# Raw weights in one tile with five places, and one split for the sums of two neighbouring quads

## The chip, the cores and the metric

The kernel runs on one core of a Trainium2 chip. The time is what the device takes for one execution, in microseconds (us). The engines work side by side, each through its own instructions in a fixed order, and wait for one another through semaphores: TensorE (PE) multiplies matrices, VectorE (DVE) and ScalarE (ACT) work element by element, GpSimd (POOL) and SyncE (SP) mostly issue DMA transfers here.

## The reference

One layer of a decoder trunk on 256 tokens of width 2048, in float32:

```
x = x + 0.5 * SwiGLU_1(RMSNorm(x))         # 2048 -> 5632 -> 2048
h = RMSNorm(x)
[attn q,k,v | m q,k,v,o,i,f] = h @ W_in    # one projection
y = concat(differential attention, mLSTM)
x = x + y @ W_out
x = x + 0.5 * SwiGLU_2(RMSNorm(x))
out = RMSNorm(x)
```

Nearly all of the work is products of activations (256 rows) with weights that are read once from memory.

## The kernel before

**Splits.** Float32 accuracy comes from two parts of each operand. A weight block `raw` is split by `split` (line 131): ACT casts it to a rounded upper half `hi` (line 132), and DVE subtracts that from the source to get the lower half `lo` (line 133). A product then takes three matmuls (`mms`, line 177): both halves of the activations with `hi` (lines 181 and 182), and the upper half of the activations with `lo` (line 184). The split weights go into pairs of tiles from the pool `wsp`, four deep.

**Seven products instead of eight.** `Paired` (line 422) multiplies the same activations with two weight arrays `wa` and `wb`. For the first `ns` pairs of contraction blocks it uses a scheme with sums in the manner of Winograd. Such a pair of blocks with its weights is called a quad here. `load` (line 440) brings three 128 x 512 pieces of a quad into a tile `raw` of the pool `wr`, which has five buffers: slot 0 from `wa`, slots 1 and 2 from `wb`. The fourth piece (`late`, line 506) comes later into another pool. The raw pieces are then added to each other in place, and between the additions the sums are split and multiplied, two quads at a time (`twos`, line 429; with an odd number the last quad is alone):

- `leading` (line 468): load; A1, the split of slot 0 as loaded; then DVE adds slots 0 and 2 to slot 1's piece (line 479, writing slots 0 and 1).
- `second_sum` (line 488): S1, the split of slot 0; then slot 2 is added to slot 0, by a DMA from POOL's queue (line 495) where `by_dma` is set and it is not the last of `twos`, by DVE otherwise (line 497).
- `sums` (line 521): S2, the split of slot 0; then POOL's queue adds `late` to slot 0 by DMA (line 533); `bare`, the split of `late`; S3, the split of slot 1.
- `second` (line 559): for each quad one split of slots 0 and 2 with a stride (line 562), the last use of the quad's buffer.

A1, S1, S2 and S3 go through `part` (line 462), which calls `split_two` (line 451): for two quads it makes two casts and two subtractions of 128 x 512, into the two halves of one pair of `wsp` tiles.

**The rest.** The contraction blocks beyond the quads are plain units: a 128 x 1024 piece from the pool `wrp` is split by one cast and one subtraction and used in twelve matmuls (`plain`, line 548). `Chain.run` (line 608) interleaves the `leading` of a Paired with the last plain units (`third`) of the one before.

**Order.** The instructions are traced under a planner that orders each engine's work by priority. Loads and splits stand 400 steps ahead of their place (`AHEAD`), so that they run ahead of the matmuls as far as buffers allow. A few copies out of the accumulators are put ahead of splits by counting splits (`ahead_of_splits`, `split_weights`, line 150). Loads of quads are issued from POOL's queue (from SP's in the first three chunks), those of plain units and of `late` from SP's.

Two more users of the pool `wr` exist, at the very start only: `tile_by_tile` (line 230) and the spare units of `load_unit` (line 212), together four buffers in the first gate product.

The Paired products in order, by number of quads: first feed-forward layer 3, 5, then two of 3, then 5, 5, two of 2, 5, 5, 5, two of 3, 5, 5, 5, two of 3; the mixing stage 2, 3, 5, 5, 5, 3 and the output projection 3, 3; second feed-forward layer 5, 5, 5, two of 3, 5, 5, two of 2, 5, 5, 5, two of 3, 5, 5, 5, two of 3.

Of the kernel before, what the change touches and what calls it, by code (L numbers as in the profile page):

```python
# [9 lines left out]
F32 = mybir.dt.float32  # L10
# [7 lines left out]
P = 128  # L18
# [6 lines left out]
CW = 512  # L25
# [7 lines left out]
UK = 2  # L33
# [10 lines left out]
AHEAD = 400  # L44
# [5 lines left out]
ON_POOL = 3  # L50
FIRST_SUMS = 3
FLUSH = 3

SEEDED = N11, N21 = "n11", "n21"

# [5 lines left out]
def tile_trunk_layer(ctx: ExitStack, tc: tile.TileContext, x, xt, par, bias_if, lamv, fnorm,  # L61
                     wg1, wu1, wd1, wqk0, wqk1, wqk2, win, wout, wg2, wu2, wd2, out):
    nc = tc.nc
# [1 line left out]
    big = ctx.enter_context(tc.tile_pool(name="big", bufs=1))  # L65
    slots = ctx.enter_context(tc.tile_pool(name="slots", bufs=22))
    work = ctx.enter_context(tc.tile_pool(name="work", bufs=8))
    wr = ctx.enter_context(tc.tile_pool(name="wr", bufs=5))
    wrp = ctx.enter_context(tc.tile_pool(name="wrp", bufs=5))
    wsp = ctx.enter_context(tc.tile_pool(name="wsp", bufs=4))  # L70
    small = ctx.enter_context(tc.tile_pool(name="small", bufs=2))
    ps_acc = ctx.enter_context(tc.tile_pool(name="ps_acc", bufs=4, space=PSUM))
    ps_tr = ctx.enter_context(tc.tile_pool(name="ps_tr", bufs=2, space=PSUM))

    wqk = [wqk0, wqk1, wqk2]
    uid = [0]

    def nm(s):
        uid[0] += 1
        return f"{s}_{uid[0]}"  # L80
# [47 lines left out]
        nc.vector.scalar_tensor_tensor(lo, src, prm[:, gcol:gcol + 1], hi.bitcast(F32),  # L128
                                       op0=ALU.mult, op1=ALU.subtract)

    def split(src, hi, lo):
        return (nc.scalar.copy(hi, src),  # L132
                nc.vector.tensor_tensor(out=lo, in0=src, in1=hi.bitcast(F32), op=ALU.subtract))  # L133


# [1 line left out]
    splits, queued = [], ([], [])  # L137

    def after(late, early):

        tc.add_manual_dep(late.ins, early.ins.name,
                          mybir.DependencyInfo(mybir.DependencyClass.NoSync, mybir.DependencyReason.DATA),
                          reason="order")
# [3 lines left out]

    ahead = ([], [])

    def split_weights(src, hi, lo):  # L150
        made = split(src, hi, lo)
        for late, q, past in zip(made, queued, ahead):
            while q and len(splits) >= q[0][0]:
                past.append(q.pop(0)[1])
            del past[:-3]
            for early in past:
                after(late, early)
        return made


    def pair_tiles(pool, tag, shape):
        return (pool.tile(shape, F32R, tag=tag + "h", name=nm(tag + "h")),
                pool.tile(shape, F32R, tag=tag + "l", name=nm(tag + "l")))
# [13 lines left out]
    def mms(jobs):  # L177


        for acc, lh, ll, rh, rl, first, last, on in jobs:  # L180
            nc.tensor.matmul(acc, lh, rh, start=first, stop=False, skip_group_check=on)  # L181
            nc.tensor.matmul(acc, ll, rh, start=False, stop=False, skip_group_check=on)  # L182
        for acc, lh, ll, rh, rl, first, last, on in jobs:
            newest[:] = [nc.tensor.matmul(acc, lh, rl, start=False, stop=last, skip_group_check=on)]  # L184
# [15 lines left out]
    def flush(n=None):  # L200

        now = pending[:n]
        del pending[:n]
        for f in now:
            f()

    def load_pair(dst, w, k, queue=nc.sync):
        queue.dma_start(dst, w[k // LK][:, k % LK:k % LK + 2, :])

    def load_unit(w, k, pieces=(UK,), spare=False):  # L210
        n = w.shape[3]
        if spare:
            raw = wr.tile([P, 3, n], F32, tag="raw", name=nm("raw"))[:, 0:UK, :]
        else:
            raw = wrp.tile([P, UK, n], F32, tag="rawp", name=nm("rawp"))
        with tc.high_priority(offset=AHEAD):
            o = k % LK
            for m in pieces:
                nc.sync.dma_start(raw[:, o - k % LK:o - k % LK + m, :], w[k // LK][:, o:o + m, :])
                o += m  # L220
        return raw
# [3 lines left out]
    def in_turn(load):  # L225
        for early in turns[-1:]:
            after(load, early)
        turns.append(load)

    def tile_by_tile(w, ahead):  # L230
        raw = wr.tile([P, 3, w.shape[3]], F32, tag="raw", name=nm("raw"))
        hi, lo = pair_tiles(wsp, "w", [P, UK, w.shape[3]])
        with tc.high_priority(offset=AHEAD):
            for t in range(UK):
                ahead(0, t)
                in_turn(nc.sync.dma_start(raw[:, t, :], w[0][:, t, :]))
                made = split_weights(raw[:, t, :], hi[:, t, :], lo[:, t, :])
        splits.append(made)
        ahead(1)
        return hi, lo  # L240

    def units(accs, xp, w, nk, last_units=1, ahead=None, w0=0, banks=None):
# [16 lines left out]
        for u in range(nu):  # L259
            if u == FLUSH:  # L260
                flush()
            if u == 0 and ahead is not None:
                rh, rl = tile_by_tile(w, ahead)
                for t in range(UK):
                    mms([(accs[hb], *halves(xp, t, hb), rh[:, t, :], rl[:, t, :], t == 0 and not (one and hb),
                          False, one) for hb in range(NT)])
                yield
                continue
            if ahead is not None and u % 2 == 0:
                ahead(u)  # L270
                ahead(u + 1)
            rh, rl = split_w(load_unit(w, w0 * LK + u * UK, (UK,), ahead is not None and u % 2 == 0), (UK,))
            if u < nu - last_units:
                products((0, 1), u, rh, rl)
            else:
                products((0,), u, rh, rl)
                tail.append((u, rh, rl))
            if u < nu - 1:
                yield
# [47 lines left out]
    A1, B1, A2, B2, S3, S1, S2, S4 = range(8)  # L327
# [7 lines left out]
    def sum_pair(xp, j, g, put_off=False):  # L335
        plain_pair(xp, j, "xs")
        split(g, *xp[j])
        (side.append if put_off else lambda f: f())(functools.partial(sums, g, xp, j))

    def sums(g, xp, j):  # L340
        s = wk("xsum").rearrange("p (a b) -> p a b", b=P)
        tt = nc.vector.tensor_tensor
        tt(out=s[:, 0:2, :], in0=g[:, 0:2, :], in1=g[:, 1:4:2, :], op=ALU.subtract)
        tt(out=s[:, 2, :], in0=s[:, 1, :], in1=g[:, 0, :], op=ALU.subtract)
        tt(out=s[:, 3, :], in0=g[:, 2, :], in1=s[:, 2, :], op=ALU.add)
        t = slots.tile([P, 2, 4, P], F32R, tag="s", name=nm("xs"))
        xp[j] += t[:, 0, :, :], t[:, 1, :, :]
        split(s, *xp[j][2:])
# [52 lines left out]
    class Early:  # L401


        def __init__(self, engine):
            self.engine = engine
# [16 lines left out]
    class Paired:  # L422

        def __init__(self, xp, wa, wb, nk, ns, w0=0, queue=nc.gpsimd, by_dma=True):

            self.queue, self.by_dma = queue, by_dma and ns > 3
            self.xp, self.wa, self.wb, self.k0 = xp, wa, wb, w0 * LK
            self.ns, self.rest = ns, range(2 * ns, nk, UK)
            self.twos = [range(j, min(j + 2, ns)) for j in range(0, ns, 2)]

            self.n = wa.shape[3]
            self.off = self.n - wb.shape[3]
            self.raws = []

        def job(self, acc, j, xi, w, wi, first, last, on=False):
            xh, xl = self.xp[j][2 * (xi // 4):][:2]
# [2 lines left out]

        def load(self, j):  # L440
            n, off = self.n, self.off
            raw = wr.tile([P, 3, n], F32, tag="raw", name=nm("raw"))
            self.raws.append(raw)
            k = self.k0 + 2 * j
            with tc.high_priority(offset=AHEAD):
                self.queue.dma_start(raw[:, 0, :], self.wa[k // LK][:, k % LK, :])
                load_pair(raw[:, 1:3, off:], self.wb, k, self.queue)
                if off:
                    nc.gpsimd.memset(raw[:, 1:3, 0:off], 0.0)

        def split_two(self, srcs):
# [7 lines left out]
                splits.append(made)  # L459
            return t  # L460

        def part(self, js, acc, xi, slot, first=False, last=False):

            t = self.split_two([self.raws[j][:, slot, :] for j in js])
            mms([self.job(acc, j, xi, t, i, first and j == 0, last and j == self.ns - 1, not first)
                 for i, j in enumerate(js)])

# [80 lines left out]
        def plain(self, w, k, accs, apart=False):  # L548

            rh, rl = split_w(load_unit(w, self.k0 + k), (UK,))  # L550

            def products(hbs):
                mms([(accs[hb], *halves(self.xp, k + t, hb), rh[:, t, :], rl[:, t, :],
                      False, k + t == self.rest[-1] + UK - 1, True) for hb in hbs for t in range(UK)])

            products((0,) if apart else (0, 1))
            return functools.partial(products, (1,))
# [481 lines left out]
    for hb in range(NT):  # L1039
        for h in range(NH):  # L1040
            i = hb * NH + h
# [226 lines left out]
```

## Time and profile before

| | |
|---|---|
| median of three runs | 1759.46 us (1758.83 to 1760.01) |
| profiled execution | 1759.56 us |
| its span, first to last instruction | 1757.8 us |
| mean granted TensorE clock | 0.999 |
| busy: PE, DVE, ACT, POOL | 1744.6, 1617.8, 1267.4, 429.3 us |
| instructions | 24486 |

Busy time is the time in which an engine has an instruction under way. A busy PE isn't PE at its peak, since matmuls are pipelined: a record is longer than the distance to the next one. Idle time of an engine that doesn't set the end costs nothing.

### The profile page before, as it was taken

To read this page: it belongs to the slowest core of one execution; us is meant where nothing else is said; L and a number is where in the kernel's file an instruction comes from. 1 tells how busy PE (TensorE), PEld (TensorE's weight loads), DVE (VectorE), ACT (ScalarE), POOL (GpSimd) and SP (SyncE) were. 2 spreads that over 40 slices of the span, in tenths; PEclk is the share of its full clock that TensorE was granted. 3 is DMA by queue.
4 is the path that set the end of the run, shared out by engine and by line. 5 is a ranking of instruction groups with operands and counts; after the bars stand their busy time and mean duration, and the time that the engine had idled before them with its cause. 6 is when DMAs were issued, how large, how long until landed. Compare 5 with 4: busy or idle time off the path is not lost.

```text
span 1757.8 us, 24486 instructions
## 1 busy us (share of the span) xinstructions
PE 1744.6 (99%) x7926; PEld 1437.7 (82%) x7926; DVE 1617.8 (92%) x2189; ACT 1267.4 (72%) x1949; POOL 429.3 (24%) x630
## 2 busy tenths in 40 slices
PE   9999999999999999999999999999999999999998
PEld 7788888888888888987888888888888878888886
DVE  7999999999999999898888999999999999999997
ACT  8666777777677768777687777776777677677765
POOL 0022332322233312012231101122332332233310
PEclk9999999999999999999999999999999999999999
DMA  9787998999799977577886667898998999799973
GB/s 365 251 254 209 259 261 265 253 292 265 218 262 258 263 252 204 185 230 221 236 238 192 209 210 211 260 265 233 258 260 268 241 268 276 232 246 256 283 254 115
DMA packets 155265, 429.72 MB, mean 244 GB/s; under 512 B 17632, under 2 KB 18944, under 8 KB 154880
## 3 DMA queue, kind: packets, MB, share of 16 engines
q0 software_dynamic: 76304, 196.66, 45.1%
q1 hardware_dynamic: 77680, 229.40, 38.0%
q10 hardware_dynamic: 1152, 2.09, 0.3%
q8 instruction: 62, 1.02, 0.2%
q14 instruction: 67, 0.55, 0.1%
HBM read 349.56 MB, written 2.10 MB: 200 GB/s over the span
## 4 chain that ended last, share of the span: by engine, by line
PE 93%; DMA 2%; DVE 2%; issue 1%; ACT 0%; POOL 0%; SPq 0%; POOLq 0%; DVEq 0%; ACTq 0%
PE acc L184 18%; PE acc L181 18%; PE acc L182 18%; PE accn L181 12%; PE accn L182 12%; PE accn L184 12%; DVE wl L133 1%; DMA raw<-in_wg_dram 1%; PE tr L373 1%; DMA raw<-in_wu_dram 1%; PE tr L314 0%; PE sc L1060 0%; DMA rawp<-in_wg_dram 0%; ACT wh L132 0%; PE num L1011 0%
## 5 line engine op out<-in xcount | busy, mean ns | idle before, releaser
L132 ACT CAST wh<-raw 128x512 fp32r<-128x512 f32 (+2 forms) x885 | 601.5, 708 | 214.5 <-PE acc L182 66.3
L133 DVE TENSOR_TENSOR wl<-raw,wh 128x512 fp32r<-128x512 f32 (+2 forms) x885 | 676.1, 793 | 58.4 <-ACT wh L132 54.5
L132 ACT CAST wh<-rawp 128x1024 fp32r<-128x1024 f32 (+3 forms) x308 | 318.2, 1035 | 109.5 <-PE acc L182 55.1
L133 DVE TENSOR_TENSOR wl<-rawp,wh 128x1024 fp32r<-128x1024 f32 (+3 forms) x308 | 367.1, 1197 | 32.0 <-ACT wh L132 29.8
L181 PE MATMUL acc<-wh,xs 128*128 128x512 f32 (+2 forms) x956 | 369.5, 387 | 0.0
L182 PE MATMUL acc<-wh,xs 128*128 128x512 f32 (+2 forms) x956 | 368.9, 386 | 0.0
L184 PE MATMUL acc<-wl,xs 128*128 128x512 f32 (+2 forms) x956 | 317.6, 387 | 0.8 <-DVE wl L133 0.7
L533 POOL DMA_DIRECT2D raw<-late x176 | 152.6, 1053 | 442.7 <-DVE wl L133 422.9
L181 PE MATMUL acc<-wh,xt 128*128 128x512 f32 (+2 forms) x564 | 218.4, 388 | 0.7 <-ACT wh L132 0.7
L182 PE MATMUL acc<-wh,xt 128*128 128x512 f32 (+2 forms) x564 | 217.3, 386 | 0.0
L181 PE MATMUL accn<-wh,xt 128*128 128x512 f32 (+1 forms) x552 | 215.3, 391 | 0.0
L182 PE MATMUL accn<-wh,xt 128*128 128x512 f32 (+1 forms) x552 | 214.7, 390 | 0.0
L479 DVE TENSOR_TENSOR raw<-raw 128x1024 f32<-128x1024 f32 x176 | 211.0, 1217 | 0.8
L184 PEld LDWEIGHTS acc<-wl,xs 128*128 128x128 f32 x956 | 178.3, 188 | 39.2 <-DVE wl L133 3.6
L181 PEld LDWEIGHTS acc<-wh,xs 128*128 128x128 f32 x956 | 179.5, 188 | 36.4 <-ACT wh L132 0.6
L182 PEld LDWEIGHTS acc<-wh,xs 128*128 128x128 f32 x956 | 179.6, 188 | 35.6
L181 PE MATMUL accn<-wh,xs 128*128 128x512 f32 (+1 forms) x408 | 162.6, 400 | 1.9 <-ACT wh L132 1.9
L182 PE MATMUL accn<-wh,xs 128*128 128x512 f32 (+1 forms) x408 | 158.0, 388 | 0.0
L184 PE MATMUL acc<-wl,xt 128*128 128x512 f32 (+2 forms) x564 | 157.6, 386 | 0.0
L495 POOL DMA_DIRECT2D raw<-raw x92 | 78.9, 899 | 322.1 <-DVE wl L133 234.7
L184 PE MATMUL accn<-wl,xt 128*128 128x512 f32 (+1 forms) x552 | 154.7, 388 | 0.0
L184 PE MATMUL accn<-wl,xs 128*128 128x512 f32 (+1 forms) x408 | 140.9, 388 | 0.0
(229 smaller groups left out, 2125.0 us busy)
## 6 DMA issues: line engine op xcount, KB each, us to landing
rawp<-in_wd_dram SPq DMA_DIRECT2D x88, 512.0 KB, 5.6
raw<-late POOLq DMA_DIRECT2D x174, 256.0 KB, 5.3
raw<-in_wu_dram POOLq DMA_DIRECT2D x80, 512.0 KB, 8.4
rawp<-in_wu_dram SPq DMA_DIRECT2D x73, 512.0 KB, 5.1
rawp<-in_wg_dram SPq DMA_DIRECT2D x69, 512.0 KB, 5.2
raw<-raw POOLq DMA_DIRECT2D x92, 256.0 KB, 4.1
raw<-in_wd_dram POOLq DMA_DIRECT2D x44, 512.0 KB, 8.6
late<-in_wg_dram SPq DMA_DIRECT2D x41, 512.0 KB, 9.2
```

The lines of the kernel that those rows point to most:

```text
L132: return (nc.scalar.copy(hi, src), nc.vector.tensor_tensor(out=lo, in0=src, in1=hi.bitcast(F32), op=ALU.subtract))
L133: nc.vector.tensor_tensor(out=lo, in0=src, in1=hi.bitcast(F32), op=ALU.subtract))
L181: nc.tensor.matmul(acc, lh, rh, start=first, stop=False, skip_group_check=on)
L182: nc.tensor.matmul(acc, ll, rh, start=False, stop=False, skip_group_check=on)
L184: newest[:] = [nc.tensor.matmul(acc, lh, rl, start=False, stop=last, skip_group_check=on)]
L373: nc.tensor.transpose(tr[:, i, hb * P:(hb + 1) * P], hs[hb][:, k * P:(k + 1) * P], ident)
L479: nc.vector.tensor_tensor(out=raw[:, 0:2, :], in0=raw[:, 0:3:2, :], in1=raw[:, 1:2, :].to_broadcast([P, 2, n]), op=ALU.add)
L495: nc.gpsimd.dma_start(raw[:, 0, :], raw[:, 2, :], accum_op=ALU.add)
L533: nc.gpsimd.dma_start(self.raws[j][:, 0, :], lates[-1][1][:, i, :], accum_op=ALU.add)
```

## The change

The pool of five raw tiles becomes one tile `ring` with five places, which go round in the order of the loads. `raw_place` counts them; the two users at the start of the kernel take places too. Where the two quads of a sum lie in places p and p+1, `part` now splits both with one operation over `ring[:, p:p+2, slot, 0:n]`, whose rows of 512 lie one place apart. Where they don't (places 4 and 0, or a quad alone), the split is as before. For A1, whose pieces come straight from the loads, the casts stay two and only the subtraction is one.

```diff
-    wr = ctx.enter_context(tc.tile_pool(name="wr", bufs=5))
+    wr = ctx.enter_context(tc.tile_pool(name="wr", bufs=1))
...
+    ring = wr.tile([P, RAWS, 3, CW], F32, name="ring")
+    turn = [0]
+
+    def raw_place():
+
+        turn[0] += 1
+        return (turn[0] - 1) % RAWS
+
+    def raw_tile(n):
+
+        return ring[:, raw_place(), :, 0:n]
...
-    def split(src, hi, lo):
-        return (nc.scalar.copy(hi, src),
+    def split(src, hi, lo, casts=1):
+        for i in range(casts - 1):
+            nc.scalar.copy(hi[:, i:i + 1, :], src[:, i:i + 1, :])
+        return (nc.scalar.copy(hi[:, casts - 1:, :], src[:, casts - 1:, :]) if casts > 1 else nc.scalar.copy(hi, src),
                 nc.vector.tensor_tensor(out=lo, in0=src, in1=hi.bitcast(F32), op=ALU.subtract))
...
-            raw = wr.tile([P, 3, n], F32, tag="raw", name=nm("raw"))
+            place = raw_place()
+            raw = ring[:, place, :, 0:n]
             self.raws.append(raw)
+            self.places.append(place)
...
+        def split_both(self, src, fresh):
+
+            with tc.high_priority(offset=AHEAD):
+                t = pair_tiles(wsp, "w", [P, 2, self.n])
+                splits.append(split_weights(src, *t, src.shape[1] if fresh else 1))
+            return t
...
-            t = self.split_two([self.raws[j][:, slot, :] for j in js])
+            at = [self.places[j] for j in js]
+            if at[-1] == at[0] + 1:
+                t = self.split_both(ring[:, at[0]:at[0] + 2, slot, 0:self.n], xi == A1)
+            else:
+                t = self.split_two([self.raws[j][:, slot, :] for j in js])
```

More of the change, by code (lines that the diff above doesn't have):

```diff
@@ L52 @@
 FLUSH = 3
+RAWS = 5
 SEEDED = N11, N21 = "n11", "n21"
@@ L148, in tile_trunk_layer, with split_weights @@
     ahead = ([], [])
-    def split_weights(src, hi, lo):
-        made = split(src, hi, lo)
+    def split_weights(src, hi, lo, casts=1):
+        made = split(src, hi, lo, casts)
         for late, q, past in zip(made, queued, ahead):
@@ L212, in load_unit @@
         if spare:
-            raw = wr.tile([P, 3, n], F32, tag="raw", name=nm("raw"))[:, 0:UK, :]
+            raw = raw_tile(n)[:, 0:UK, :]
         else:
@@ L230, in tile_by_tile @@
     def tile_by_tile(w, ahead):
-        raw = wr.tile([P, 3, w.shape[3]], F32, tag="raw", name=nm("raw"))
+        raw = raw_tile(w.shape[3])
         hi, lo = pair_tiles(wsp, "w", [P, UK, w.shape[3]])
@@ L432, in __init__ @@
             self.off = self.n - wb.shape[3]
-            self.raws = []
+            self.raws, self.places = [], []
         def job(self, acc, j, xi, w, wi, first, last, on=False):
```

## The prediction

> **What bounds the kernel now.** I read the page's sums first, then the chain of waits, then the busy times by stretch, and then the places where TensorE (PE) waits.
>
> ```profile
> PE 1744.6 (99%) x7926; PEld 1437.7 (82%) x7926; DVE 1617.8 (92%) x2189; ACT 1267.4 (72%) x1949; POOL 429.3 (24%) x630
> ...
> PE 93%; DMA 2%; DVE 2%; issue 1%; ACT 0%; POOL 0%; SPq 0%; POOLq 0%; DVEq 0%; ACTq 0%
> ```
>
> PE is busy for 99% of the span and carries 93% of the chain that ended last. VectorE (DVE) comes second with 92%. The busy times by stretch show where PE's missing 13 us lie (columns: length, then the busy time of each engine with its instructions, the granted clock, the DMA share and rate):
>
> ```profile
> 0.00:12.00 12.00, 8.80 (x28) 4.73 (x29) 5.51 (x12) 7.11 (x12) 1.92 (x13) 1.00 0.76 269
> 12.00:1748.80 1736.80, 1735.32 (x7898) 1432.95 (x7898) 1609.58 (x2170) 1257.72 (x1933) 426.67 (x616) 1.00 0.84 244
> 1748.80:1757.80 9.00, 0.45 (x2) 0.02 (x1) 2.66 (x8) 2.56 (x7) 0.67 (x1) 0.72 0.66 233
> ```
>
> Head and tail hold 11.75 us of PE's idle time (12.00 - 8.80 and 9.00 - 0.45). Neither has a split of sums in it. In the 1736.80 us between, PE idles 1.48 us (1736.80 - 1735.32). That is a little too kind, because a matmul's record lasts longer than the distance to the next one. The PE timeline at one of the few holes shows it (start, duration, engine, line):
>
> ```profile
> 1415.91 0.39 PE L182 MATMUL acc<-wh,xs 128*128 128x512 f32 x1
> 1416.14 0.39 PE L184 MATMUL acc<-wl,xs 128*128 128x512 f32 x1
> 1417.06 0.50 PE L184 MATMUL acc<-wl,xs 128*128 128x512 f32 x1 [0.54 <-DVE wl L133]
> ...
> 1602.22 0.39 PE L184 MATMUL acc<-wl,xs 128*128 128x512 f32 x1
> 1602.77 0.50 PE L184 MATMUL acc<-wl,xs 128*128 128x512 f32 x1 [0.17 <-DVE wl L133]
> ```
>
> Starts are 0.23 us apart when nothing is late (1415.91, 1416.14). So the first hole costs 0.92 - 0.23 = 0.69 us where 0.54 is shown as idle, and the second costs 0.55 - 0.23 = 0.32 us. About 0.16 us per hole has to be added to the idle time. Who waited for whom says how many holes the splits make (us in total, times, longest):
>
> ```profile
> PEld acc L184 <- DVE wl L133: 4.9, 13, 1.0
> PE accn L181 <- ACT wh L132: 1.9, 3, 0.9
> PEld accn L181 <- ACT wh L132: 3.7, 3, 1.8
> PE acc L184 <- DVE wl L133: 0.7, 2, 0.5
> ```
>
> That is about 20 holes, some of the ScalarE (ACT) ones in the head. The bound on what faster splits can give back is therefore 1.48 + 20 x 0.16 = 4.7 us.
>
> **The change part by part.** First, how many pairs it reaches. The places go round modulo five, in the order of the loads. The first gate product takes four, so the quads start at place 4. A Paired with quads at 2, 3, 4, 0, 1 has the pairs (2,3) and (4,0): the second wraps and keeps its two operations. Going through the Paired of both feed-forward layers and the mixing stage in order (quads 3, 5, 3, 3, 5, 5, 2, 2, 5, 5, 5, 3, 3, 5, 5, 5, 3, 3; then 2, 3, 5, 5, 5, 3, 3, 3; then 5, 5, 5, 3, 3, 5, 5, 2, 2, 5, 5, 5, 3, 3, 5, 5, 5, 3, 3) gives 22 neighbours of 27 pairs, 6 of 11, and 23 of 30: 51 of 68. The quads add up to 70 + 29 + 77 = 176, which is the count of the row of line 479 below. All 51 are 512 wide, because the one narrow pair wraps.
>
> Each pair is split in four sums (A1, S1, S2 and S3). The prices stand in the groups by form; the rows with 128x1024 from raw are today's split with a stride (slots 0 and 2, line 562), so the strided operand is in the trace:
>
> ```profile
> L132 ACT CAST wh<-raw 128x512 fp32r<-128x512 f32 x698 | 410.5, 622 | 203.3 <-PE acc L182 57.2 <-DVE raw L479 44.7 <-DMA raw<-in_wg_dram 42.2
> ...
> L132 ACT CAST wh<-raw 128x1024 fp32r<-128x1024 f32 x177 | 185.4, 1054 | 8.4 <-PE acc L182 8.0 <-DMA raw<-in_wg_dram 0.2 <-ACT cv L410 0.2
> ...
> L133 DVE TENSOR_TENSOR wl<-raw,wh 128x512 fp32r<-128x512 f32 x698 | 456.2, 686 | 49.1 <-ACT wh L132 45.4 <-PE acc L184 2.7
> L133 DVE TENSOR_TENSOR wl<-raw,wh 128x1024 fp32r<-128x1024 f32 x177 | 213.9, 1221 | 9.0 <-ACT wh L132 9.0
> L479 DVE TENSOR_TENSOR raw<-raw 128x1024 f32<-128x1024 f32 x174 | 209.0, 1220 | 0.8
> ```
>
> DVE: 2 x 686 - 1221 = 151 ns less per merged split; 51 x 4 x 151 ns = 30.8 us, and 204 instructions fewer. ACT: 2 x 622 - 1054 = 190 ns less in S1, S2 and S3, nothing in A1, which keeps two casts; 51 x 3 x 190 ns = 29.1 us and 153 instructions fewer. Matmuls, loads and the queues that issue them stay as they are. A place is free again when the last split of its slots 0 and 2 (line 562) is through, as a buffer was, so I cost the tile with five places itself at nothing; what hides any difference is that ACT is held back by PE, not by loads:
>
> ```profile
> ACT wh L132 <- PE acc L182: 137.3, 197, 2.2
> DVE wl L133 <- ACT wh L132: 86.9, 169, 2.7
> ACT wh L132 <- DMA raw<-in_wg_dram: 42.4, 31, 3.6
> ...
> ACT wh L132 <- DMA raw<-raw: 6.6, 14, 1.2
> ```
>
> ACT waits for PE to give back split buffers 197 times, against 31 + 14 waits for data. So the 30.8 and 29.1 us come off engines that run ahead of PE, and almost all of it turns into longer waits for PE. What reaches the end is only what fills a hole, or makes one.
>
> *What fills.* Before the hole at 1417.06 three merged splits stand in DVE's order (A1 of both pairs and S1 of the first; all places there are neighbours): 3 x 0.151 = 0.45 us of its 0.69 us. I take -0.45, between 0 and -0.69.
>
> *What it costs.* A merged split is gated by its later half. With empty queues, today's first lower half is there after 622 + 686 = 1308 ns and the second after 1308 + 686 = 1994 ns; merged, both come after 1054 + 1221 = 2275 ns, which is +0.97 and +0.28 us. In A1 the two casts stay, and DVE waits for the second. The stretch of the other hole shows what that means (ACT, then DVE):
>
> ```profile
> 1593.64 0.62 ACT L132 CAST wh<-raw 128x512 fp32r<-128x512 f32 x1 [1.05 <-DMA raw<-in_wg_dram]
> 1597.89 0.62 ACT L132 CAST wh<-raw 128x512 fp32r<-128x512 f32 x1 [3.62 <-DMA raw<-in_wg_dram]
> ...
> 1595.48 0.68 DVE L133 TENSOR_TENSOR wl<-raw,wh 128x512 fp32r<-128x512 f32 x1
> 1598.55 0.69 DVE L133 TENSOR_TENSOR wl<-raw,wh 128x512 fp32r<-128x512 f32 x1 [2.38 <-ACT wh L132]
> 1599.15 1.22 DVE L479 TENSOR_TENSOR raw<-raw 128x1024 f32<-128x1024 f32 x1
> ```
>
> The first quad of the pair landed 4 us before the second, and DVE did the first's split in idle time. Merged, that work moves behind the second's cast: 1221 - 686 = 0.53 us later, and behind it in DVE's order wait two operations of line 479, for them ACT's casts of S1, and the matmuls at 1602.77. I take +0.53 here, between 0 and +0.53. Elsewhere the later half is covered by the plain units that PE works through meanwhile (twelve matmuls, 12 x 0.23 = 2.8 us each). I take 0; if that cover is gone it is the second rival below.
>
> *Sum.* -0.45 + 0.53 = +0.1 us on a profiled execution of 1759.56 us (span 1757.8 us and 1.76 us around it). That execution lies 0.1 us over the median of the runs, 1759.46 us, so the forecast is **1759.5 us**. A measurement of this kernel can tell about 0.2%, 3.5 us, from no change.
>
> The Trainium skill (Perfetto Trace Analysis, Identifying the Most-Contended Engine) says to distrust matmul busy time, to judge TensorE by the busy share of its weight loads, and to take the engine with the highest occupancy as the one that limits. Here that would be DVE, 92% against 82%, and the time would fall with DVE's. That is the first rival; the rows of starts 0.23 us apart speak against the rule.
>
> **The rivals.**
>
> *DVE is the bound.* If PE only kept step with DVE, the 30.8 us would come off the end: 1759.5 - 30.8 = 1728.7 us. For it speaks 92% of busy DVE. Against it: DVE's own waits for ACT (86.9 us), and PE's 1.48 us of idle time in the middle, from which no 30.8 us can come. 3%.
>
> *All holes close.* DVE and ACT gain enough reserve that PE never waits: -4.7 us, 1754.8 us. Against it: the holes in the head are ACT's first casts, which stay. 12%.
>
> *The pair's second half becomes the wait (slower).* In S1 the result of each quad releases its own addition by DMA (line 495), and S2 reads what that wrote. Around the second pair of the stretch after 1417 (POOL's issues; ACT; DVE):
>
> ```profile
> 1419.64 0.85 POOL L495 DMA_DIRECT2D raw<-raw  x1 [1.47 <-DVE wl L133]
> 1421.38 0.84 POOL L495 DMA_DIRECT2D raw<-raw  x1 [0.89 <-DVE wl L133]
> ...
> 1426.26 0.62 ACT L132 CAST wh<-raw 128x512 fp32r<-128x512 f32 x1 [1.20 <-DMA raw<-raw]
> 1426.91 0.69 DVE L133 TENSOR_TENSOR wl<-raw,wh 128x512 fp32r<-128x512 f32 x1 [1.30 <-ACT wh L132]
> ```
>
> Today the two additions go out 1.74 us apart, each after its own split. Merged, both are released together, at best when the second is today plus 0.28 us, and the second's issue stands behind the first's 0.85 us: some 1.1 us later. The merged S2 then ends 0.97 us later still than the second half does today: 2.1 us in all. Where PE has less reserve than that, it waits. With 14 waits of this kind today and no reserve at any, the cost is 14 x 2.1 = 29 us; a quarter of them gives +7 us, 1766.5 us. It decides from two such places on (4.2 us). For it: DVE already waits 1.30 us here. Against it: 14 waits sum to only 6.6 us, and the places where PE itself runs out are few. 24%.
>
> *The places are not kept apart.* If a strided read counted as everything from its first to its last word, S3's split of slot 1 would also wait for the additions into slot 0 of the next place (line 533), and PE would miss, for example, the six matmuls of a pair, 6 x 0.23 = 1.4 us, at 51 pairs: +70 us, 1830 us. No row speaks for it, and the trace of before can't show it, since each place is a tile of its own there. 3%.
>
> **How the numbers follow.** No change that can be told, at 1759.5 us with its own range of 1756 to 1763: 58%. All holes close 12% and DVE as the bound 3%: faster 15%. The pair's second half 24% and places not kept apart 3%: slower 27%. The range 1755 to 1767 reaches the closed holes and the quarter of the late halves, and leaves out the two far rivals and the outer parts of the near ones, together under 20%.
>
> **What would show it.** Right: PE x7926 as before; DVE x1985 and ACT x1796; DVE's 128x512 from raw at 698 - 408 = 290 and 128x1024 at 381; ACT's at 392 and 330; means within 10 ns of 686, 1221, 622 and 1054; DVE some 31 us and ACT some 29 us less busy, and ACT's waits for PE longer by about as much. Wrong: PE's middle stretch idle by more than 5 us; ACT's waits for line 495's additions grown from 6.6 us to tens (the third rival); or a span shorter by more than 5 us (DVE as the bound).

## The result and the profile after

The change makes the kernel slower: 1791.66 us (median of five runs, 1789.39 to 1794.95) against 1760.01 us for the kernel before beside it (1758.83 to 1762.59). The ratio is 1.0178, with a 95% interval from 1.0164 to 1.0192. The profiled span is 1788.2 us, 30.4 us more than before.

In the changed kernel the cast of `split` is line 147 (the first of A1's two casts is line 146), the subtraction line 148. The three matmuls are lines 196, 197 and 199, the sum of slots line 507, the addition by DMA line 523, and that of `late` line 561. A raw tile is called `ring`.

The page's sums and its chain of waits, after:

```profile
PE 1759.4 (98%) x7926; PEld 1434.8 (80%) x7926; DVE 1605.3 (90%) x1985; ACT 1251.2 (70%) x1796; POOL 429.0 (24%) x630
...
PE 77%; DMA 9%; DVE 6%; issue 5%; ACT 2%; POOL 1%; SPq 0%; DVEq 0%; POOLq 0%; ACTq 0%
```

PE issues the same 7926 matmuls, but its share of the chain falls from 93% to 77%; DMA has 9% of it and DVE 6%, both 2% before. Of DMA's 9% the page gives 5% to loads of quads (`ring<-in_wg_dram`) and 3% to the additions. ACT's waits for these loads didn't grow, though: 42.4 us before, 37.6 us on line 147 and 6.1 us on line 146 after. The middle stretch, after:

```profile
12.00:1779.20 1767.20, 1750.63 (x7899) 1430.17 (x7898) 1597.23 (x1966) 1241.73 (x1780) 426.38 (x616) 1.00 0.83 240
```

PE idles 1767.20 - 1750.63 = 16.57 us here, 1.48 us before; each hole costs some more than its idle time, as in the prediction. So 15.1 of the 30.4 us stand as idle time of PE; the other 15.3 us are in its busy time, with the same number of matmuls. Who waited for whom, after (us in total, times, longest):

```profile
DVE wl L148 <- ACT wh L147: 133.6, 178, 4.8
ACT wh L147 <- PE acc L197: 128.1, 164, 4.0
...
ACT wh L147 <- DMA ring<-ring: 35.6, 26, 4.9
PEld acc L199 <- DVE wl L148: 23.9, 51, 1.4
PEld acc L196 <- ACT wh L147: 13.7, 14, 2.1
```

ACT's waits for the additions by DMA grew from 6.6 us (14 times) to 35.6 us (26 times), DVE's waits for ACT from 86.9 to 133.6 us, and PE's weight loads (PEld) now wait for lower halves 51 times instead of 13.

One place shows the mechanism. It is the same product in both kernels, the one whose hole at 1602.77 us the prediction shows. After the change: POOL's additions, the merged S2 on ACT and DVE, and PE (one fence for each engine's timeline):

```profile
1629.00 0.90 POOL L523 DMA_DIRECT2D ring<-ring  x1 [2.00 <-DVE wl L148]
1633.12 1.72 POOL L523 DMA_DIRECT2D ring<-ring  x2 [3.23 <-DVE wl L148]
```

```profile
1640.11 1.04 ACT L147 CAST wh<-ring 128x1024 fp32r<-128x1024 f32 x1 [4.89 <-DMA ring<-ring]
```

```profile
1641.19 1.23 DVE L148 TENSOR_TENSOR wl<-ring,wh 128x1024 fp32r<-128x1024 f32 x1 [4.69 <-ACT wh L147]
```

```profile
1639.06 0.61 PE L199 MATMUL acc<-wl,xs 128*128 128x512 f32 x2
1641.20 0.50 PE L196 MATMUL acc<-wh,xs 128*128 128x512 f32 x1 [1.53 <-ACT wh L147]
```

Before the change, POOL and ACT at the same place:

```profile
1605.35 0.84 POOL L495 DMA_DIRECT2D raw<-raw  x1 [1.44 <-DVE wl L133]
1607.09 0.85 POOL L495 DMA_DIRECT2D raw<-raw  x1 [0.89 <-DVE wl L133]
```

```profile
1609.68 0.62 ACT L132 CAST wh<-raw 128x512 fp32r<-128x512 f32 x1 [0.24 <-DMA raw<-raw]
```

The two additions of the pair went out 1.74 us apart, and ACT waited 0.24 us. Now both go out together after the merged S1. The chain has the wait for the later one's landing, 1633.66 us plus 6.35 us:

```profile
1633.66 6.35 DMA ring<-ring
```

The merged S2 then waits 4.89 us on ACT, everything behind it on ACT and DVE waits as well, and PE stands still for 1.53 us. The landing takes long here: the median of all additions of this kind is 4.4 us after the change and 4.1 us before. Why it is longer at this place was not followed.

The hole has a second price here. Behind it, for 3.41 us, TensorE's granted clock is 0.50, and matmuls start 0.43 us apart instead of 0.23 us. PE's timeline, and the busy times of that stretch (the clock is the third number from the end):

```profile
1643.43 0.63 PE L196 MATMUL accn<-wh,xs 128*128 128x512 f32 x1
1643.85 0.63 PE L197 MATMUL accn<-wh,xs 128*128 128x512 f32 x1
```

```profile
1642.56:1645.97 3.41, 3.41 (x8) 2.69 (x9) 3.41 (x5) 2.61 (x6) 1.93 (x3) 0.50 0.57 94
```

At half the clock, PE loses half of the 3.41 us, 1.7 us. It is the only such stretch between the start and the tail, and the kernel before has none, so some 1.7 us of this execution's 30 us are the clock's.

The groups by form, after:

```profile
L147 ACT CAST wh<-ring 128x1024 fp32r<-128x1024 f32 x330 | 346.2, 1053 | 97.7 <-DMA ring<-ring 33.2 <-PE acc L197 32.4 <-DVE ring L507 8.1
L147 ACT CAST wh<-ring 128x512 fp32r<-128x512 f32 x341 | 206.2, 620 | 135.6 <-DVE ring L507 43.3 <-DMA ring<-in_wg_dram 37.4 <-PE acc L197 29.1
```

```profile
L148 DVE TENSOR_TENSOR wl<-ring,wh 128x1024 fp32r<-128x1024 f32 x381 | 462.7, 1221 | 93.3 <-ACT wh L147 90.6 <-PE acc L197 1.0
...
L148 DVE TENSOR_TENSOR wl<-ring,wh 128x512 fp32r<-128x512 f32 x290 | 193.8, 685 | 13.3 <-ACT wh L147 10.9 <-PE acc L199 1.3 <-DMA ring<-in_win_dram 0.8
```

Counts and means are as worked out (ACT's 341 and the 51 first casts of A1 make 392). The merged operations were made at the pairs that were meant, and each lasts as long as forecast; what is lost is lost in waiting.

### The profile page after: what moved, and what is told of

Same layout as the page of the kernel before. It is cut to its first block, busy times and chain, and to the rows that moved or that the text cites. A ratio compares the mean times of both kernels' runs of the same rounds, so it can differ in the third digit from the quotient of the medians.

```text
span 1788.2 us, 24079 instructions
## 1 busy us (share of the span) xinstructions
PE 1759.4 (98%) x7926; PEld 1434.8 (80%) x7926; DVE 1605.3 (90%) x1985; ACT 1251.2 (70%) x1796; POOL 429.0 (24%) x630
## 4 chain that ended last, share of the span: by engine, by line
PE 77%; DMA 9%; DVE 6%; issue 5%; ACT 2%; POOL 1%; SPq 0%; DVEq 0%; POOLq 0%; ACTq 0%
PE acc L199 15%; PE acc L196 14%; PE acc L197 14%; PE accn L196 10%; PE accn L197 10%; PE accn L199 10%; DMA ring<-in_wg_dram 5%; DVE wl L148 4%; DMA ring<-ring 3%; ACT wh L147 1%; PE tr L388 1%; DVE ring L507 1%; DMA late<-in_wd_dram 1%; POOL ring L523 0%; DMA rawp<-in_wqk_dram 0%
## 5 line engine op out<-in xcount | busy, mean ns | idle before, releaser
L148 DVE TENSOR_TENSOR wl<-ring,wh 128x512 fp32r<-128x512 f32 (+2 forms) x681 | 657.4, 984 | 106.6 <-ACT wh L147 101.5
L147 ACT CAST wh<-ring 128x512 fp32r<-128x512 f32 (+2 forms) x681 | 554.8, 829 | 234.4 <-PE acc L197 61.9
L561 POOL DMA_DIRECT2D ring<-late x176 | 152.4, 1056 | 480.4 <-DVE wl L148 441.7
L507 DVE TENSOR_TENSOR ring<-ring 128x1024 f32<-128x1024 f32 x176 | 209.4, 1217 | 1.8
L523 POOL DMA_DIRECT2D ring<-ring x92 | 79.4, 988 | 325.2 <-DVE wl L148 320.1
```

Source lines behind the costliest of these rows:

```text
L147: return (nc.scalar.copy(hi[:, casts - 1:, :], src[:, casts - 1:, :]) if casts > 1 else nc.scalar.copy(hi, src), nc.vector.tensor_tensor(o ...
L507: nc.vector.tensor_tensor(out=raw[:, 0:2, :], in0=raw[:, 0:3:2, :], in1=raw[:, 1:2, :].to_broadcast([P, 2, n]), op=ALU.add)
L523: nc.gpsimd.dma_start(raw[:, 0, :], raw[:, 2, :], accum_op=ALU.add)
L561: nc.gpsimd.dma_start(self.raws[j][:, 0, :], lates[-1][1][:, i, :], accum_op=ALU.add)
```

## The experiments

The first four take the change apart: the tile alone, and the merging of single sums. `xi` is the sum that `part` makes.

**The tile alone.**

```diff
-            if at[-1] == at[0] + 1:
+            if False and at[-1] == at[0] + 1:
```

> One tile with five places, but every sum split quad by quad as before (no merged operation). If the merged splits are to blame for the 31 us, this runs like the kernel before: 1760 us, within 3 us, DVE x2189 and ACT x1949. If the tile with places is to blame (loads or additions that wait for a neighbouring place), it runs like the changed kernel: about 1790 us.

Measured: 1763.35 us, ratio 1.0023 (1.0013 to 1.0032). The tile with places costs some 3 us of the 31; the merged splits cost the rest. Part of the 3 us lies near the start: this kernel, like the others with the tile, has holes near 48 us and near 54 us (0.7 us of idle time each) where the kernel before has a single one near 52 us. SP's queue issues two loads for quads there ahead of two loads of plain units, where the kernel before issues them behind. That this makes the second hole, and what the rest is, was not tried. All that follows is compared with this kernel too. Its profile is of the slowest of its ten runs (1768.96 us), so its waits are, if anything, on the high side.

**Only A1 merged.**

```diff
-            if at[-1] == at[0] + 1:
+            if at[-1] == at[0] + 1 and xi == A1:
```

> Of the merged splits only A1's (two casts, one subtraction that waits for both loads). Theory 'late load' (the second quad's load gates the first quad's subtraction and the additions behind it): most of the loss is here, 1775 to 1790 us. Theory 'late addition' (S1, whose result releases the additions by DMA that S2 reads): little of it is here, 1760 to 1768 us.

Measured: 1765.16 us, ratio 1.0028 (1.0016 to 1.0039), 1.8 us over the tile alone, which is within the noise. The gate on the second quad's load, from which I took my only cost, is nearly free. "Late load" falls as the main cause.

**Only S1 merged** (`and xi == S1`).

> Of the merged splits only S1's (one cast, one subtraction). Theory 'late addition': both additions by DMA go out together and later, S2's casts wait for them (tens of us instead of 6.6), 1772 to 1788 us. Theory 'late load': 1758 to 1764 us.

Measured: 1774.38 us, ratio 1.0076 (1.0053 to 1.0098), 11 us over the tile alone. ACT's waits for the additions by DMA, first in the tile alone and then here:

```profile
ACT wh L147 <- DMA ring<-ring: 7.7, 12, 1.8
```

```profile
ACT wh L147 <- DMA ring<-ring: 22.4, 24, 2.5
```

They double in number and triple in length, as "late addition" has it.

**S2 and S3 merged** (`and xi in (S2, S3)`).

> Of the merged splits only S2's and S3's. S3 reads what has been ready for long, S2 what the additions by DMA wrote. Theory 'late addition': S2's wait for the second addition costs some, 1762 to 1770 us. Theory 'late load': 1756 to 1762 us, perhaps a little faster than before, since DVE and ACT have less to do.

Measured: 1774.60 us, ratio 1.0078 (1.0063 to 1.0093), 11 us over the tile alone: more than either theory said. So the next runs took S2 and S3 apart, and asked where, and in which operation, the loss lies.

**Only the products without additions by DMA** (all four sums merged there).

```diff
-            if at[-1] == at[0] + 1:
+            if at[-1] == at[0] + 1 and not self.by_dma:
```

> All four sums merged, but only in the products whose additions DVE makes (down projections, output projection, the small projections); the products of five quads, with additions by DMA, split quad by quad. Theory 'late half' (loads, additions by DMA and the reserve of the long products decide): no loss beyond that of the tile with places, 1761 to 1765 us. Theory 'order' (any change of the order in which ACT and DVE work costs): a loss in proportion, 24 of 51 pairs and so 1772 to 1776 us.

Measured: 1764.16 us, ratio 1.0025 (1.0015 to 1.0035), as the tile alone. These merges are free within the noise; the loss comes from the long products with additions by DMA. The pairs merged here are 17 of the 51 and not the 24 of the expectation: DVE has 2121 instructions, 4 x 17 fewer than without merging. In proportion that would still have been some 9 us (17/51 of the 28.3 us that separate the changed kernel from the tile alone), so "order" falls all the same.

**Only S2 merged** (`and xi == S2`).

> Of the merged splits only S2's. Theory 'late half': S2's first half waits for the second addition by DMA, so nearly all of the 11 us that S2 and S3 cost together over the tile with places lies here: 1770 to 1776 us. Theory 'order': about half of it, 1767 to 1770 us.

Measured: 1773.09 us, ratio 1.0069 (1.0052 to 1.0086), 10 us over the tile alone. The waits for the additions, here:

```profile
ACT wh L147 <- DMA ring<-ring: 21.2, 19, 2.2
```

**Only S3 merged** (`and xi == S3`).

> Of the merged splits only S3's, whose inputs were ready long before. Theory 'late half': as the tile with places alone, 1761 to 1765 us. Theory 'order': about half of the 11 us that S2 and S3 cost together, 1767 to 1770 us.

Measured: 1762.19 us, ratio 1.0008 (0.9998 to 1.0017). S3's inputs have long been there, and its merge costs nothing: it is the same operation as S2's, at as many places. The waits for the additions stay as they were:

```profile
ACT wh L147 <- DMA ring<-ring: 6.5, 10, 1.5
```

**One cast, two subtractions** in S1, S2 and S3; A1 as before.

```diff
+        cast = nc.scalar.copy(hi, src)
+        for i in range(casts):
+            at = slice(i, i + 1) if casts > 1 else slice(None)
+            sub = nc.vector.tensor_tensor(out=lo[:, at], in0=src[:, at], in1=hi[:, at].bitcast(F32), op=ALU.subtract)
+        return cast, sub
...
-            if at[-1] == at[0] + 1:
+            if at[-1] == at[0] + 1 and xi != A1:
```

> S1, S2 and S3 with one cast for both quads, but two subtractions; A1 as before. If the late subtraction of the first quad is what costs (its lower half and the addition behind it), this gives most of it back: 1763 to 1770 us. If the one cast that waits for both quads is what costs, it stays: 1775 to 1788 us.

Measured: 1772.43 us, ratio 1.0070 (1.0055 to 1.0085), 9 us over the tile alone, a little above the range for "most of it given back". The cast that waits for both quads has a share of its own, since ACT's queue stands behind it:

```profile
ACT wh L145 <- DMA ring<-ring: 31.0, 21, 4.0
```

**Two casts in all four sums, one subtraction.**

```diff
-                splits.append(split_weights(src, *t, src.shape[1] if fresh else 1))
+                splits.append(split_weights(src, *t, src.shape[1]))
```

> The changed kernel (1791.7 us) with two casts in all four merged sums, so that ACT works as it does before the change and only DVE's subtraction is one for both quads. One cast with two subtractions cost 9 us over the tile with places. If both halves of the merge cost alike through the second quad's lateness: 1774 to 1784 us. If the subtraction is what matters: 1784 to 1792 us.

Measured: 1797.25 us, ratio 1.0211 (1.0196 to 1.0226), slower than the change and outside both ranges. By these two runs the subtraction for both quads is the dearer half. One cast has both upper halves after 1053 ns, two casts after 2 x 620 = 1240 ns. So the subtraction starts still later here, which fits; that this is the cause was not tried by itself. Part of the difference to the changed kernel is the clock: this profile has three stretches of 3.41 us at 0.50, 5.1 us lost against 1.7 us.

**One addition by DMA for the pair**, on the kernel with only S1 merged.

```diff
+                if self.by_dma and at[-1] == at[0] + 1:
+                    p = slice(at[0], at[0] + 2)
+                    nc.gpsimd.dma_start(ring[:, p, 0, 0:self.n], ring[:, p, 2, 0:self.n], accum_op=ALU.add)
+                    return
```

> As s1_alone (1774 us; only S1 merged), but the additions of slot 2 to slot 0 of both quads go out as one DMA of 512 KB instead of two of 256 KB, so that the second doesn't stand behind the first's issue of some 0.85 us. Theory 'late addition' (S2's casts wait for the second addition): the waits for it and the time fall by a part, 1766 to 1772 us, unless the larger DMA lands later by as much. If the merge costs through DVE's and ACT's order and not through the additions: 1774 us as before.

Measured: 1780.44 us, ratio 1.0116 (1.0095 to 1.0136), 6 us slower than with two additions. The reservation of the expectation came true, and more: the larger addition lands later (median 5.7 us against 4.7), and S2 of the first quad waits for all of it. From the list of DMA issues and from the waits:

```profile
ring<-ring POOLq DMA_DIRECT2D x34, 512.0 KB, 5.7
```

```profile
ACT wh L147 <- DMA ring<-ring: 40.2, 23, 4.1
```

Against S1 alone, time and waits for the additions rise together once more. Across all runs they don't: 40.2 us of waits here go with 1780 us, 35.6 us in the changed kernel with 1792 us. The waits show that a chain is late; they don't add up to what PE loses.

**One plain unit moved** to stand between S1 and S2, in the changed kernel and, as the control, in the kernel before.

```diff
-                while done < min(self.steps - 1, -(-(i + 1) * self.steps // (q + 1))):
+                while done < min(self.steps - 1, -(-(i + 1) * self.steps // (q + 1)) - (i > 0)):
```

> The changed kernel with the plain units of the product before moved back: one more of them (twelve matmuls, 2.8 us) stands between S1 of the last pair and S2, one less ahead of it. The splits and their merging stay. Theory 'late addition' (PE's cover between S1 and S2 is too short by 1 to 3 us): most of the loss from S1 and S2 goes, 1766 to 1780 us. If the loss comes from elsewhere: 1788 us or more.

> The kernel before with the same move of one plain unit, as the control: its additions land in time, so more cover gives it nothing. Both theories: 1758 to 1766 us, no faster than before beyond the holes that it has now (under 5 us).

Measured: 1809.52 us, ratio 1.0277 (1.0262 to 1.0292), and 1775.53 us, ratio 1.0085 (1.0066 to 1.0104). Both expectations failed. The control shows why nothing follows for the theory: without any merge the move alone costs 15 us, and its waits for the additions, too, rose from 6.6 us to

```profile
ACT wh L132 <- DMA raw<-raw: 20.6, 23, 3.3
```

So the move takes cover away somewhere, and whether it lengthened the time between S1 and its use at all was not read. What it shows is that moving a unit at this place costs the kernel before 15 us by itself. In the changed kernel the clock adds to it: 20.5 us at 0.50 in that profile, up to 10 us lost.

**Lateness without a merge.** So far a merged operation was always both: late for its first quad, and longer. The last three runs merge nothing. On the tile with places, at the same neighbouring pairs, the second quad is split ahead of the first.

```diff
...
-                    for i, src in enumerate(srcs):
+                    for i, src in (reversed if swap else list)(list(enumerate(srcs))):
...
-            if at[-1] == at[0] + 1:
+            if False and at[-1] == at[0] + 1:
...
-                t = self.split_two([self.raws[j][:, slot, :] for j in js])
+                t = self.split_two([self.raws[j][:, slot, :] for j in js], at[-1] == at[0] + 1 and xi == S2)
```

> The tile with places, nothing merged; in S2 of neighbouring quads the second quad is split ahead of the first, so that the first waits for the second's addition by DMA as it does in a merged S2. Theory 'lateness': a good part of what a merged S2 costs over the tile with places (9.7 us) comes back without any merging, 1768 to 1775 us. Theory 'length and order of operations': as the tile with places alone, 1762 to 1766 us.

> The same for S1: the second quad is split ahead of the first, whose addition by DMA goes out first on POOL's queue, so that both additions wait for both subtractions as with a merged S1 (11 us over the tile with places). Theory 'lateness': 1768 to 1775 us. Theory 'length and order': 1762 to 1766 us.

> The same in A1, S1, S2 and S3 at once, 51 pairs each, with the operations of the kernel before. Theory 'lateness': most of the change's 31 us without any merging, 1775 to 1792 us. Theory 'length and order': 1762 to 1768 us.

Measured: S2 swapped 1773.26 us, ratio 1.0073 (1.0056 to 1.0089); S1 swapped 1773.02 us, ratio 1.0072 (1.0054 to 1.0091); all four swapped 1772.50 us, ratio 1.0082 (1.0050 to 1.0113). The waits for the additions, in S2 swapped and then in S1 swapped:

```profile
ACT wh L147 <- DMA ring<-ring: 23.0, 18, 2.9
```

```profile
ACT wh L147 <- DMA ring<-ring: 24.9, 21, 2.5
```

Each of the two alone costs what its merge costs (1773.26 against 1773.09 us; 1773.02 against 1774.38 us), with the operations of the kernel before and, in S2, the same order of operations on ACT, DVE and the queues as with the tile alone; in S1 the order differs at a few places on ACT and DVE. Lateness is shown as the cause for S2, and for S1 with that small reservation. All four swapped together miss their range: 12 us and not the 31. Swapped throughout, the second quad leads in every sum, and the waits for the additions are short again. The waits for the loads of quads are little longer than with the tile alone (47.3 us, 33 times), so what makes the 9 us over the tile alone here stays open:

```profile
ACT wh L147 <- DMA ring<-in_wg_dram: 50.3, 28, 4.9
...
ACT wh L147 <- DMA ring<-ring: 8.9, 14, 1.2
```

**What the parts make together.** Tile 3.1 us, A1 1.8, S1 11.0, S2 9.7, S3 -1.2 (the last four over the tile alone): 24.4 us of the 31.7 between the medians. Some 7 us come only when the merges act together; by the ratios, which don't go by medians, it is some 12 us. The clock has 1.7 us of that in the profiled execution. An S1 that releases later and an S2 that needs both are links of one chain, which would account for more; this was not tried, and no run merges S1 and S2 without the others.

## Why the prediction was wrong

**What bounds the kernel: right.** PE set the end before, and judging by busy shares would have misled. DVE's busy time fell by 12.5 us and ACT's by 16.2 us, and the kernel got 31 us slower.

**Pairs and instructions: right.** 51 pairs of 68, DVE x1985, ACT x1796, the four group counts and the means all came out. (The row of line 479 that the prediction shows has 174 of its 176 quads; the other two are the narrow pair.)

**The saving: its size was wrong.** Forecast were 30.8 us less on DVE and 29.1 us less on ACT; 12.5 and 16.2 us came. The term 2 x 686 - 1221 took mean durations, but operations in a row overlap. The timeline of DVE and that of ACT in the kernel before:

```profile
535.13 2.35 DVE L479 TENSOR_TENSOR raw<-raw 128x1024 f32<-128x1024 f32 x2
...
550.49 1.90 DVE L133 TENSOR_TENSOR wl<-raw,wh 128x512 fp32r<-128x512 f32 x3 [0.25 <-ACT wh L132]
```

```profile
288.97 2.00 ACT L132 CAST wh<-rawp 128x1024 fp32r<-128x1024 f32 x2
...
549.83 1.67 ACT L132 CAST wh<-raw 128x512 fp32r<-128x512 f32 x3
```

Three of 686 ns take 1.90 us, so the next one starts (1.90 - 0.69) / 2 = 0.60 us after the last; of 1221 ns it is 2.35 - 1.22 = 1.13 us. That makes 2 x 0.60 - 1.13 = 0.07 us per merged subtraction, 204 x 0.07 = 14 us. For ACT it is (1.67 - 0.62) / 2 = 0.53 us and 2.00 - 1.05 = 0.95 us, so 0.11 us and 153 x 0.11 = 17 us. It changed little, as the forecast put the gain at 0.45 us. ACT's waits for PE, which were to grow by as much as was saved, stayed where they were: 137.3 us before, 128.1 us on line 147 and 11.1 us on line 146 after.

**The cost of lateness: the step that failed.** "Elsewhere the later half is covered by the plain units that PE works through meanwhile [...]. I take 0" was the wrong term. In the products without additions by DMA it held (1764.16 us); in the long ones the cover wasn't enough. I priced A1 (+0.53 us), which turned out to cost under 2 us, and put S1 and S2, 11 and 10 us, at nothing.

**The third rival was what happened.** It named the additions released together, the later S2, and 2.1 us per place; its full price, 14 waits x 2.1 = 29 us, is close to what was measured, but that is luck: the waits became 26, and S1 and S2 merged by themselves make only 21 us. I took a quarter of the price and gave it 24%. Against it I held that the 14 waits summed to only 6.6 us. That was a misreading: here a wait that is short and comes often marked a chain that arrives just in time, and a delay put into it reached the end. The first rival (DVE) and the second (all holes close) fell. The fourth fell as well: places that aren't kept apart would have shown in S3 alone, at its price of 70 us.

**The observables:** PE's idle time in the middle (over 5 us) and the waits for the additions (to tens of us) were named as signs of the third rival, and both came.

## What to carry to other kernels

One operation over two pieces of data starts when the later piece is there, and its first result comes when both are done. Merging cost nothing where both inputs had long been ready (S3, the products without additions by DMA), though what it gained there is within the noise; it isn't worth it where one piece's result releases the next step, here an addition by DMA that is read again a few us later. Before costing such a delay at nothing, look for waits in that chain: here 14 short waits were the sign that it had no slack, while PE was busy for 99% of the span.

## What the runs showed of the hardware

Operations in a row on one engine overlap in the records. A 128x512 subtraction of 686 ns takes 0.60 us of DVE when another follows, and one of 128x1024, of 1221 ns, takes 1.13 us; merging two saves 0.07 us and not the 0.15 us that the means suggest. An addition by DMA of 512 KB landed 1.0 us later in the median than one of 256 KB (5.7 against 4.7 us), so that here, where the first half is read first, two small ones were the better choice.

A hole on TensorE can cost more than its length. In the changed kernel the granted clock was 0.50 for 3.41 us behind one of them, with matmuls 0.43 us apart. Not every hole did this: with S1 alone merged, PE had one of 1.6 us, and the clock stayed at 1.00 up to the tail.
